# Block products of the last feed-forward ahead of every second weight tile, and fold loads one job earlier

## The chip, the cores and the metric

The kernel runs on one core of one Trainium2 chip. A core has TensorE (PE, matmuls), VectorE (DVE), ScalarE (ACT), GpSimd (POOL) and SyncE (SP); each takes its instructions in a fixed order of its own, and they wait for one another by semaphores. Sixteen DMA engines move data between HBM and the on-chip memory SBUF; matmul results lie in PSUM. Times are microseconds (us) of the device for one execution; the time of a kernel is the median of several executions.

## The reference

A two-layer encoder over 272 tokens (16 meta tokens and 256 real ones) of width 2048, in float32. Each layer has an attention branch, a Fourier branch, gates, and a convolutional feed-forward of width 5632:

```
for i in range(DEPTH):                       # DEPTH = 2
    h = _rmsnorm(h_stream, norm_mix[i])
    proj = h @ w_in[i]                       # q | k | v | f | ga | gf
    ...
    h_stream = h_stream + merged @ w_out[i]
    h2 = _rmsnorm(h_stream, norm_ffn[i])
    up = h2 @ w_up[i]                        # 2048 -> 2 * 5632
    u_gate = _dwconv3_centred(up[..., :D_FF], w_conv[i], b_conv[i])
    u_val = up[..., D_FF:]
    h_stream = h_stream + (jax.nn.silu(u_gate) * u_val) @ w_down[i]
return h_stream[:, N_META:]
```

## The kernel before

**Weight tiles.** All weights pass through the core once, in chunks of 512 KB, numbered in the order of their use. SP loads a chunk into a buffer `raw` (`load_raw`, L264; four buffers, and up to two more, `raw5`). To get float32 accuracy from PE's shorter format, `split_w` makes two parts of it: ACT casts it to `wh` (L306), and DVE makes `wl`, the chunk minus `wh` (L308). There are three buffers each of `wh` and `wl`. `next_split` brings the splits two chunks ahead of the one that PE uses. The activations are split in the same way, into a and b, and PE adds up wh·a, wh·b and wl·a. A buffer is free when PE has used it for the last time.

**Weight tiles and products.** `group` (L377 to L379) uses a chunk as a *weight tile*: 24 matmuls, 272 columns wide, or 258 in the last feed-forward (in its few `uv` groups 16, L373 and L374, half of them twice as wide). The last feed-forward (layer 1) mixes these with *block products*: the value half of `up` and the down projection are worked out by block formulas that save multiplications and use sums and differences of weights, prepared earlier and kept in HBM. `products` (L1467) uses a chunk as a product: six matmuls 512 columns wide, four with `wh`, two with `wl`. There are 252 of them. The small operands of products, `opnd`, are made from activations (`make`, `split_unit`) by a cast on ACT (L1315) and a difference on DVE (L1316), at times after sums (L1401, L1405, L1407, L1525, L1526); there are two buffers of them. Finished sums of products are handed out of PSUM by L1386, L1446 or L1448.

**The gate.** Each `ug` group has four weight tiles, and at its end stands `conv_gate`: for each of two halves `u` (DVE L1302), then the convolution (ACT L1304, DVE L1306 and L1307), then silu (ACT L1308); where the value half comes from products, four small transposes on PE (L1502, `ps_vr`) and two multiplications on DVE (L1504) follow.

**What sets the order.** The 120 chunks of the `ug`, `uv` and `t` groups of the last feed-forward are counted by t. A table of due numbers says how many products must have been begun by which t, and `mix` stands that many ahead of a tile:

```
DUE = ((0, 0), (7, 0), (43, 96), (62, 112), (64, 112), (98, 196), (100, 196), (118, 252), (120, 252))
```

Between the points of the table it goes in a straight line: two or three products ahead of every tile, fewer than one for t from 43 to 62. Side work is cut into steps: after every second group of matmuls `step` issues the next piece of the generators that stand in line (`push(generator, wait)`; the number that a generator yields is the steps until its next piece). The order in which an engine takes its instructions is then fixed by a planner that looks at the whole program, and may bring some rows of an engine forward where it reckons with a wait; what it did is seen in the rows below.

**Folds.** In the feed-forward of layer 0, `prepare` makes folded weights for layer 1: POOL loads a chunk (`wi`, L541), DVE makes eight sums and differences of its blocks into `wo` (L540), POOL stores `wo` to HBM (`fw`). A job has seven steps; the load of job n is issued two jobs ahead of its work. Loads and results take turns in seven buffers. Later jobs of the same loop (sums) have their loads four jobs ahead.

**Key statistics.** In layer 1, `kstats` runs beside the `v` group: sums of squares (PE `ps_ss`, DVE L948), a power on POOL (L518), `dk` on DVE (L994), and `ps_kb` on PE (L997).

Of the kernel before, what the change touches and what calls it, by code (L numbers as in the profile page):

```python
# [10 lines left out]
F32 = mybir.dt.float32  # L11
# [5 lines left out]
P = 128  # L17
# [15 lines left out]
CW = 4  # L33
MG = 2
# [127 lines left out]
def encoder_kernel(ctx, tc, xT, params, consts, bmat, cfold, csign, w_fl, w_f64c, w_in, w_abr, w_four, w_f64, w_out, w_up, w_down, w_vn, w_dn, w_dt, out):  # L162
# [13 lines left out]
    for l in range(DEPTH):  # L176
# [13 lines left out]
        for half in range(2):  # L190
            for kind, j in BRANCH_ORDER[half]:
                w, off, n = {"ga": (w_in, IN_GA, KT), "gf": (w_in, IN_GF, KT), "s": (w_four, 0, 8), "a": (w_abr, 0, 8)}[kind]
# [20 lines left out]
    def due(t):  # L213
        (t0, d0), (t1, d1) = next(v for v in zip(DUE, DUE[1:]) if v[0][0] <= t < v[1][0])
        return d0 + (d1 - d0) * (t - t0) // (t1 - t0)

    chunks, folded, streamed, mix, summed, stage, small_w = [], set(), set(), {}, {}, {}, {}
    t, done = 0, 0
    for key, chs in order:
        for j, ch in enumerate(chs):  # L220
            n = 0
            if key[0] == 1 and key[1] in ("t", "ug", "uv"):
                n = due(t) - done
                t += 1
            if n:
                mix[key, j] = n
                for s, p, k in PRODUCTS[done:done + n]:
                    if p in (3, 4, 5, 6):
                        summed[len(chunks)] = (min(s, len(VSETS)), (3, 0, 1, 2)[p - 3], k)
                    streamed.add(len(chunks))  # L230
                    chunks.append(pchunks[done])
                    done += 1
                first_mix = min(first_mix, len(chunks) - n) if done > n else len(chunks) - n
            if key[:2] == (0, "s"):
                folded.add(len(chunks))
            if key[:2] == (1, "t"):
                streamed.add(len(chunks))
            if key[1] in BRANCH:
                stage[len(chunks)] = key[0]
                if key[1] == "gf" and j == 0:  # L240
                    small_w[len(chunks) + KT // CW] = (key[0], key[2])
            chunks.append(ch)
# [71 lines left out]
    def push(gen, wait=0):  # L314
        shadow.append([wait, gen])
# [197 lines left out]
    def bc2(ap):  # L513
        return _rep(ap, 2)

    def pow_half(out, src):
        n = src.shape[1]
        nc.gpsimd.tensor_tensor(out, src, mhalf[:, :n], op=ALU.pow)  # L518
# [20 lines left out]
    def prepare(pool):  # L539
        tt = lambda *v, **kw: tc.keep_in_program_order(nc.vector.tensor_tensor(*v, **kw))  # L540
        dma = lambda *v: tc.keep_in_program_order(nc.gpsimd.dma_start(*v))  # L541
        tile_ = lambda n: pool.tile([P, CW, MG * P], F32, tag="ws", name=n, bufs=7)
        folds = [(w_fl[k], k) for k in range(KT)] + [(w_four[1, j, c], KT + 2 * j + c) for j in range(NG) for c in range(2)]
        sums = []
        for s_, f, wd, nq in ((0, fv[0], w_vn[0], NV), (len(VSETS), ft, w_dn, NQ)):
            for k in range(nq):
                sums += [(wd[h, nq * e + k], (s_, f, q, k)) for h, e, q in ((0, 0, 0), (1, 0, 2), (1, 1, 1), (0, 1, 3))]

        def fold(held, n, j):
            a, o = held[n], tile_(f"wo{n}")  # L550
            for q, op in ((0, ALU.add), (1, ALU.subtract)):
                for c in range(2):
                    half = (lambda t_, e: t_[:, 2 * c:2 * c + 2, e * P:(e + 1) * P]) if j < KT else (lambda t_, e: t_[:, 2 * e + c])
                    tt(half(o, q), half(a, 0), half(a, 1), op=op)
                    yield 1
            dma(fw[j], o)

        def sum_up(held, n, s_, f, q, k):
            x, y = held[n], held[n + (1, -2, 1, -1)[q]]
            for c in (0, 2):  # L560
                tt(x[:, c:c + 2], x[:, c:c + 2], y[:, c:c + 2], op=ALU.add)
                yield 1
            dma(f[q, k], x)
            ready_sums.add((s_, q, k))

        for jobs, ahead, work in ((folds, 2, lambda h, n, to: fold(h, n, to)), (sums, 4, lambda h, n, to: sum_up(h, n, *to))):
            held = {}
            for n in range(len(jobs) + ahead):
                if n < len(jobs):
                    held[n] = tile_(f"wi{n}")  # L570
                    dma(held[n], jobs[n][0])
                left = 7 - n % 4 // 3
                if n >= ahead:
                    for v in work(held, n - ahead, jobs[n - ahead][1]):
                        left -= v
                        yield v
                yield left
# [56 lines left out]
    for l in range(DEPTH):  # L634
        last = l == DEPTH - 1
# [6 lines left out]
        with tc.tile_pool(name=f"mix{l}", bufs=1) as mp:  # L642
# [23 lines left out]
            def ut(name):  # L666
                return mp.tile([P, T], F32, tag="u", name=name, bufs=2)
# [275 lines left out]
            def sums_t(dst, blocks):  # L943
                n = len(blocks)
                ss = psum.tile([P, 512], F32, tag="aux", name="ps_ss")
                for i in range(n):
                    nc.tensor.transpose(ss[:, i * P:(i + 1) * P], blocks[i], ident)
                nc.vector.tensor_reduce(dst, ss[:, 0:n * P].rearrange("p (i n) -> p i n", i=n), axis=AX.X, op=ALU.add)  # L948

            def swap(hp):  # L950
                qs = rt("qs")
                for b in range(4):
                    tc.keep_in_program_order(nc.sync.dma_start(qs[32 * b:32 * b + 32, :, :], hp[32 * (b ^ 1):32 * (b ^ 1) + 32, :, :]))
                return qs
# [6 lines left out]
            def rope(hp, qs, H, L):  # L961
                turn(hp, qs)
                nc.scalar.copy(H, hp)
                yield 1
                nc.vector.tensor_tensor(L, hp, H.bitcast(F32), op=ALU.subtract)
# [16 lines left out]
            def kstats():  # L982
                kss = small.tile([P, 2, 3], F32, tag="kss", name="kss")
                for m in range(NKV):
                    sums_t(kss[:, m, :], (kms[m], ksq[:, m, 16:144], ksq[:, m, 144:272]))
                nc.vector.tensor_tensor(kss, kss, bc2(tok2), op=ALU.mult)
                nc.vector.tensor_scalar(kss, kss, 1.0 / HD, EPS, op0=ALU.mult, op1=ALU.add)
                rk = small.tile([P, 2, 3], F32, tag="rk", name="rk")
                pow_half(rk.rearrange("p a b -> p (a b)"), kss.rearrange("p a b -> p (a b)"))
                yield 4 if last else 6  # L990
                for kv in range(NKV):
                    dk = ut("dk")
                    for i, (a, b) in enumerate(BLK):
                        nc.vector.tensor_scalar(dk[:, a:b], mask[:, a:b], rk[:, kv, i:i + 1], None, op0=ALU.mult)  # L994
                    yield 5
                    pk = psum.tile([P, 512], F32, tag="aux", name="ps_kb")
                    nc.tensor.matmul(pk[:, :T], ones, dk, start=True, stop=True)  # L997
                    nc.vector.tensor_tensor(kp[:, kv, :], kp[:, kv, :], pk[:, :T], op=ALU.mult)
                yield 3
                qs = swap(kp)  # L1000
                yield 8
                yield from rope(kp, qs, kH, kL)
                hold["keys"] = True

            push(kstats(), 6 if last else 4)
            if last:
                slots = fold_setup()
                push(fold_ahead(slots), 2)
# [186 lines left out]
            for i in range(4):  # L1195
# [3 lines left out]
                if last:  # L1199
                    if i in (0, 2):  # L1200
                        until(hold, "vt" if i == 0 else "fold")
                        for t_, n in ((qH, "q1"), (qL, "q2")):
                            o = Q_AT[l][t_ is qL][i // 2]
                            t = mp.tile([P, 4 * T + o], F32R, tag=n + "ab"[i // 2], name=n)
                            t_.append(t[:, o:o + 4 * T].rearrange("p (h t) -> p h t", t=T))
                elif i == 0:
                    until(hold, "vt")
                    until(hold, "fold")
                    for t_, n in ((qH, "q1"), (qL, "q2")):
                        o = Q_AT[l][t_ is qL][0]  # L1210
                        t = mp.tile([P, NH * T + o], F32R, tag=n, name=n)[:, o:o + NH * T].rearrange("p (h t) -> p h t", t=T)
# [74 lines left out]
        with tc.tile_pool(name=f"ffn{l}", bufs=1) as fp:  # L1286
# [3 lines left out]
            if not last:  # L1290
                slow[2] = 0
                push(prepare(fp), 8)
# [334 lines left out]
```

## Time and profile before

| | |
|---|---|
| median of 3 runs | 2507.89 us (2507.48 to 2508.49) |
| profiled execution | 2508.71 us, its span 2506.9 us |
| PE busy | 2497.2 us |
| DVE busy | 1987.6 us |
| ACT busy | 1340.5 us |
| POOL busy | 205.5 us |

The span runs from the first to the last instruction that the profile shows; 1.8 us of the profiled execution lie outside it. "Busy" counts the time in which an engine works on at least one instruction. A row of the timeline gives the start in the span, the duration, the engine, the line of the kernel, the operation with output and inputs, how many instructions stand in the row, and in brackets the idle time before it with what ended that. Durations of neighbouring rows may overlap, since an engine begins an instruction before the last one has fully ended. In the list of waits a row gives the waiting instruction, what it waited for, and the us in total, the number of times and the longest.

### The profile page before, as it was taken

Reading aid. Unit: us, or ns where it says so; the run is one execution under the profiler, and the core shown is the slowest. Engines: PE = TensorE matmul, PEld = TensorE weight load, DVE = VectorE, ACT = ScalarE, POOL = GpSimd, SP = SyncE. Lnnn points to the kernel's source line nnn. Section 1 sums busy time; section 2 is a strip of 40 time slices with the busy share of each in tenths; the row PEclk is TensorE's granted clock in tenths of the full one; section 3 lists DMA queues with packets and bytes.
Section 4 is the critical chain, followed back from the end, with each engine's and each line's share of the span. In section 5 each row is a group of like instructions: output and inputs, shape, how many; then the busy total and the mean of one; then the engine's idle time right before and its main releaser. Section 6 shows DMA issues by size and latency. Waiting matters only on the chain.

```text
span 2506.9 us, 47935 instructions
## 1 busy us (share of the span) xinstructions
PE 2497.2 (100%) x18848; PEld 2417.8 (96%) x18848; DVE 1987.6 (79%) x3155; ACT 1340.5 (53%) x1913; POOL 205.5 (8%) x394
## 2 busy tenths in 40 slices
PE   9999999999999999999999999999999999999999
PEld 9999999999999999999999999999988899999887
DVE  7687866778878667888778887666888787898898
ACT  6455444554444334444445555444676665666665
POOL 0000000012212222222200000000000000000000
PEclk9999999999999999999999999999999999999999
DMA  6544557879999999999975547888778886788887
GB/s 249 167 153 166 189 194 243 264 261 377 386 338 381 396 388 385 391 383 389 386 282 200 199 153 241 267 259 272 246 266 293 296 294 236 262 283 290 280 302 272
DMA packets 194803, 706.85 MB, mean 282 GB/s; under 512 B 22145, under 2 KB 27393, under 8 KB 194321
## 3 DMA queue, kind: packets, MB, share of 16 engines
q1 hardware_dynamic: 146768, 517.09, 58.0%
q0 software_dynamic: 46368, 184.57, 21.2%
q8 instruction: 147, 2.41, 0.4%
q10 hardware_dynamic: 1440, 2.13, 0.2%
q14 instruction: 80, 0.65, 0.1%
HBM read 623.32 MB, written 111.15 MB: 293 GB/s over the span
## 4 chain that ended last, share of the span: by engine, by line
PE 98%; DMA 1%; DVE 1%; issue 0%; ACT 0%; POOL 0%; SPq 0%; DVEq 0%
PE ps_p L1467 14%; PE ps_ug L379 7%; PE ps_ug L377 7%; PE ps_ug L378 7%; PE ps_d L379 3%; PE ps_d L377 3%; PE ps_d L378 3%; PE ps_uv L379 3%; PE ps_uv L377 3%; PE ps_uv L378 3%; PE ps_gf L377 3%; PE ps_ga L377 2%; PE ps_ga L378 2%; PE ps_o L379 2%; PE ps_o L377 2%; PE ps_ga L379 2%
## 5 line engine op out<-in xcount | busy, mean ns | idle before, releaser
L306 ACT CAST wh<-raw 128x1024 fp32r<-128x1024 f32 (+1 forms) x961 | 998.3, 1044 | 885.1 <-PE ps_ug L378 201.7
L308 DVE TENSOR_TENSOR wl<-raw,wh 128x1024 fp32r<-128x1024 f32 (+1 forms) x961 | 1159.0, 1217 | 388.6 <-ACT wh L306 378.4
L377 PE MATMUL ps_ug<-xHL,wh 128*128 128x272 f32 (+1 forms) x1408 | 400.4, 285 | 0.0
L379 PE MATMUL ps_ug<-xHL,wl 128*128 128x272 f32 (+1 forms) x1408 | 398.7, 284 | 0.0
L378 PE MATMUL ps_ug<-xHL,wh 128*128 128x272 f32 (+1 forms) x1408 | 398.5, 283 | 0.0
L377 PEld LDWEIGHTS ps_ug<-xHL,wh 128*128 128x128 f32 x1408 | 264.9, 188 | 3.2
L378 PEld LDWEIGHTS ps_ug<-xHL,wh 128*128 128x128 f32 x1408 | 264.5, 188 | 3.2
L379 PEld LDWEIGHTS ps_ug<-xHL,wl 128*128 128x128 f32 x1408 | 264.3, 188 | 1.1 <-DVE wl L308 0.4
L1467 PE MATMUL ps_p<-wh,opnd 128*128 128x512 f32 x816 | 222.1, 392 | 0.0
L379 PE MATMUL ps_uv<-xHL,wl 128*128 128x272 f32 x704 | 202.0, 287 | 0.7 <-DVE wl L308 0.7
L379 PE MATMUL ps_d<-gHL,wl 128*128 128x272 f32 x704 | 201.7, 287 | 0.0
L377 PE MATMUL ps_uv<-xHL,wh 128*128 128x272 f32 x704 | 201.3, 286 | 0.0
L377 PE MATMUL ps_d<-gHL,wh 128*128 128x272 f32 x704 | 201.1, 286 | 0.0
L378 PE MATMUL ps_uv<-xHL,wh 128*128 128x272 f32 x704 | 200.6, 285 | 0.0
L378 PE MATMUL ps_d<-gHL,wh 128*128 128x272 f32 x704 | 200.6, 285 | 0.0
L1467 PEld LDWEIGHTS ps_p<-wh,opnd 128*128 128x128 f32 x816 | 148.3, 188 | 28.7 <-ACT wh L306 0.2
L377 PE MATMUL ps_ga<-xHL,wh 128*128 128x272 f32 (+1 forms) x512 | 147.8, 289 | 0.0
L540 DVE TENSOR_TENSOR wi<-wi,wi 128x512 f32<-128x512 f32 x224 | 147.0, 685 | 0.0
L377 PE MATMUL ps_gf<-xHL,wh 128*128 128x272 f32 (+1 forms) x512 | 146.8, 287 | 0.0
L379 PE MATMUL ps_o<-mH,wl 128*128 128x272 f32 (+1 forms) x512 | 145.8, 285 | 0.0
L377 PE MATMUL ps_o<-mH,wh 128*128 128x272 f32 (+1 forms) x512 | 145.5, 284 | 0.0
L378 PE MATMUL ps_ga<-xHL,wh 128*128 128x272 f32 (+1 forms) x512 | 145.4, 284 | 0.0
(381 smaller groups left out, 5957.8 us busy)
## 6 DMA issues: line engine op xcount, KB each, us to landing
raw<-in_w_up SPq DMA_DIRECT2D x288, 512.0 KB, 6.4
raw<-in_w_in SPq DMA_DIRECT2D x191, 512.0 KB, 3.7
raw<-in_w_down SPq DMA_DIRECT2D x88, 512.0 KB, 7.1
wi<-in_w_dn POOLq DMA_DIRECT2D x80, 512.0 KB, 9.6
ft<-wi POOLq DMA_DIRECT2D x80, 512.0 KB, 7.8
raw<-ft SPq DMA_DIRECT2D x80, 512.0 KB, 4.5
raw<-in_w_out SPq DMA_DIRECT2D x64, 512.0 KB, 4.2
raw<-fv SPq DMA_DIRECT2D x64, 512.0 KB, 4.6
```

The costliest lines, as they stand in the source:

```text
L306: nc.scalar.copy(h[:, a:b], r[:, a:b])
L308: nc.vector.tensor_tensor(lo[:, a:b], r[:, a:b], h[:, a:b].bitcast(F32), op=ALU.subtract)
L377: nc.tensor.matmul(o, h[:, c, sl], a, start=kt == 0, stop=False)
L378: nc.tensor.matmul(o, h[:, c, sl], b, start=False, stop=False)
L379: nc.tensor.matmul(o, lo[:, c, sl], a, start=False, stop=kt == nk - 1)
L540: tt = lambda *v, **kw: tc.keep_in_program_order(nc.vector.tensor_tensor(*v, **kw))
L1467: nc.tensor.matmul(ps[h], x, w[:, 512 * h:512 * h + 512], start=fresh and (s_, q) in BEGIN and first, stop=(s_, q) in END and end, skip_gr ...
```

## The change

In the last feed-forward, the number of products ahead of a tile is now taken for two tiles at once: ahead of an even t stand those due at t + 1, ahead of an odd t none. Where the table rises fastest this makes five to seven ahead of every even tile in place of two or three ahead of each. The total stays 252.

Loads of folds are issued three jobs ahead of their work in place of two; since the work keeps its distance to the load by this count, the work of a fold and its store come one job later. The buffers for it are nine in place of seven. In the key statistics of layer 1, the first piece comes after 5 steps in place of 6, and the wait behind it is 5 in place of 4, so the later pieces keep their place.

```
@@ the order of chunks
             n = 0
             if key[0] == 1 and key[1] in ("t", "ug", "uv"):
-                n = due(t) - done
+                n = due(t + 1 - t % 2) - done
                 t += 1
@@ prepare
-        tile_ = lambda n: pool.tile([P, CW, MG * P], F32, tag="ws", name=n, bufs=7)
+        tile_ = lambda n: pool.tile([P, CW, MG * P], F32, tag="ws", name=n, bufs=9)
...
-        for jobs, ahead, work in ((folds, 2, lambda h, n, to: fold(h, n, to)), (sums, 4, lambda h, n, to: sum_up(h, n, *to))):
+        for jobs, ahead, work in ((folds, 3, lambda h, n, to: fold(h, n, to)), (sums, 4, lambda h, n, to: sum_up(h, n, *to))):
@@ kstats
-                yield 4 if last else 6
+                yield 5 if last else 6
...
-            push(kstats(), 6 if last else 4)
+            push(kstats(), 5 if last else 4)
```

Below, tiles go by their number in the order of use (`wh806` and `wl806` are the two parts of chunk 806); the number behind the underscore is only the planner's.

DVE in the last feed-forward, at the end of `ug` group 16. Before, 803 and 807 are weight tiles, 804 to 806 and 808 are products:

```order
L308 TENSOR_TENSOR wl804_26863<-raw804_26717,wh804_26862 128x1024
L1504 TENSOR_TENSOR act_22652<-cv_26825,ps_vr_26830 128x256
L308 TENSOR_TENSOR wl805_26877<-raw805_26747,wh805_26876 128x1024
L1525 TENSOR_TENSOR XT_70<-act_22652 128x256
L1526 TENSOR_TENSOR act_22652<-act_22652 128x2x128
L308 TENSOR_TENSOR wl806_26905<-raw806_26759,wh806_26904 128x1024
L1316 TENSOR_TENSOR opnd_26910<-XT_70,opnd_26910 128x256
L308 TENSOR_TENSOR wl807_26920<-raw807_26774,wh807_26919 128x4x256
L308 TENSOR_TENSOR wl808_26932<-raw808_26786,wh808_26931 128x1024
```

Now 801 to 805 are products, 806 and 807 weight tiles, and the next products begin with 808:

```order
L308 TENSOR_TENSOR wl804_26863<-raw804_26717,wh804_26862 128x1024
L1504 TENSOR_TENSOR act_22652<-cv_26825,ps_vr_26830 128x256
L308 TENSOR_TENSOR wl805_26875<-raw805_26729,wh805_26874 128x1024
L1525 TENSOR_TENSOR XT_70<-act_22652 128x256
L1316 TENSOR_TENSOR opnd_26880<-XT_70,opnd_26880 128x256
L1526 TENSOR_TENSOR act_22652<-act_22652 128x2x128
L308 TENSOR_TENSOR wl806_26890<-raw806_26744,wh806_26889 128x4x256
L308 TENSOR_TENSOR wl807_26902<-raw807_26756,wh807_26901 128x4x256
```

The splits of 804 and 805 keep their place; the operand of the products from 808 on (`opnd_26910`, now `opnd_26880`), made from what L1525 writes, now comes ahead of the split of 806.

ACT at the same place, before:

```order
L306 CAST wh804_26862<-raw804_26717 128x1024
L1315 CAST opnd_26853<-act_22652 128x256
L306 CAST wh805_26876<-raw805_26747 128x1024
L1308 ACTIVATE cv_26825<-cv_26825 128x256
L306 CAST wh806_26904<-raw806_26759 128x1024
L306 CAST wh807_26919<-raw807_26774 128x4x256
L1315 CAST opnd_26910<-XT_70 128x256
L306 CAST wh808_26931<-raw808_26786 128x1024
```

and now:

```order
L306 CAST wh804_26862<-raw804_26717 128x1024
L306 CAST wh805_26874<-raw805_26729 128x1024
L1308 ACTIVATE cv_26825<-cv_26825 128x256
L1315 CAST opnd_26880<-XT_70 128x256
L306 CAST wh806_26889<-raw806_26744 128x4x256
L306 CAST wh807_26901<-raw807_26756 128x4x256
L306 CAST wh808_26921<-raw808_26786 128x1024
```

The cast of the operand moved from behind the casts of 806 and 807 to ahead of both.

PE at the end of group 17. Before, 832 to 834 are products, 835 a weight tile:

```order
L1467 MATMUL ps_p10_22999<-wh834_27469,opnd_27333 128x512
L1467 MATMUL ps_p11_23000<-wh834_27469,opnd_27333 128x512
L1467 MATMUL ps_p10_22999<-wh834_27469,opnd_27333 128x512
L1467 MATMUL ps_p11_23000<-wh834_27469,opnd_27333 128x512
L1467 MATMUL ps_p10_22999<-wl834_27470,opnd_27333 128x512
L1467 MATMUL ps_p11_23000<-wl834_27470,opnd_27333 128x512
L377 MATMUL ps_1_ug_14_0_27402<-xHL_71,wh835_27481 128x258
L378 MATMUL ps_1_ug_14_0_27402<-xHL_71,wh835_27481 128x258
L377 MATMUL ps_1_ug_14_1_27403<-xHL_71,wh835_27481 128x258
L378 MATMUL ps_1_ug_14_1_27403<-xHL_71,wh835_27481 128x258
L379 MATMUL ps_1_ug_14_0_27402<-xHL_71,wl835_27482 128x258
```

Now 829 to 833 are products, 834 and 835 weight tiles, and the next products begin with 836:

```order
L377 MATMUL ps_1_ug_14_0_27402<-xHL_71,wh834_27451 128x258
L378 MATMUL ps_1_ug_14_0_27402<-xHL_71,wh834_27451 128x258
L377 MATMUL ps_1_ug_14_1_27403<-xHL_71,wh834_27451 128x258
L378 MATMUL ps_1_ug_14_1_27403<-xHL_71,wh834_27451 128x258
L1502 MATMUL ps_vr_27658<-cst_73,vR_22653 128x128
L1502 MATMUL ps_vr_27658<-cst_73,vR_22655 128x128
L1502 MATMUL ps_vr_27658<-cst_73,vR_22653 128x128
L1502 MATMUL ps_vr_27658<-cst_73,vR_22655 128x128
L1467 MATMUL ps_p10_22999<-wl833_27440,opnd_27303 128x512
L1467 MATMUL ps_p11_23000<-wl833_27440,opnd_27303 128x512
L1467 MATMUL ps_p10_22999<-wh836_27481,opnd_27429 128x512
L1467 MATMUL ps_p11_23000<-wh836_27481,opnd_27429 128x512
```

The four `wh` matmuls of the weight tile, the transposes and two matmuls of the next product now stand ahead of its first `wl` matmul, which follows. At group 16 it goes in the same way: two matmuls of weight tile 806 stand ahead of the `wl` part of 805, two behind it, then three transposes and the four `wh` matmuls of 808.

POOL at the beginning of the folds, before:

```order
L541 DMA wi2_6943<-in_w_fl 128x1024
L541 DMA fw_66<-wo0_6945 128x1024
L541 DMA wi3_7005<-in_w_fl 128x1024
L541 DMA fw_66<-wo1_7007 128x1024
L541 DMA wi4_7063<-in_w_fl 128x1024
L541 DMA fw_66<-wo2_7065 128x1024
L541 DMA wi5_7125<-in_w_fl 128x1024
```

and now:

```order
L541 DMA wi2_6943<-in_w_fl 128x1024
L541 DMA wi3_6999<-in_w_fl 128x1024
L541 DMA fw_66<-wo0_7001 128x1024
L541 DMA wi4_7057<-in_w_fl 128x1024
L541 DMA fw_66<-wo1_7059 128x1024
L541 DMA wi5_7119<-in_w_fl 128x1024
```

Each load now stands ahead of one store more.

## The prediction

> **What bounds the kernel now.** I read the head of the page first, then the chain of waits, then the list of what TensorE (PE) waited for, and last the windows by stage.
>
> ```profile
> span 2506.9 us, 47935 instructions
> PE 2497.2 (100%) x18848; PEld 2417.8 (96%) x18848; DVE 1987.6 (79%) x3155; ACT 1340.5 (53%) x1913; POOL 205.5 (8%) x394
> PEclk9999999999999999999999999999999999999999
> PE 98%; DMA 1%; DVE 1%; issue 0%; ACT 0%; POOL 0%; SPq 0%; DVEq 0%
> ```
> ```profile
> PE ps_f L444 <- ACT wh L306: 4.5, 1, 4.5
> PE ps_uv L379 <- DVE wl L308: 0.7, 1, 0.7
> PE ps_kb L997 <- DVE dk L994: 0.5, 1, 0.5
> PE ps_uv L374 <- DVE wl L308: 0.3, 1, 0.3
> ```
> ```profile
> 1826.00:2042.00 216.00, 215.68 (x1226) 188.48 (x1225) 180.83 (x218) 149.44 (x185) 0.00 (x0) 1.00 0.85 291
> 2090.00:2330.00 240.00, 240.00 (x1573) 219.63 (x1572) 206.11 (x273) 155.76 (x197) 0.00 (x0) 1.00 0.79 270
> ```
>
> PE is the whole span: 2497.2 of 2506.9 us, 98% of the chain, always at full clock. In the list of waits only the last row lies in the last feed-forward. In the windows (columns: length, busy PE, weight loads, VectorE (DVE), ScalarE (ACT), GpSimd (POOL), clock, DMA share, GB/s) PE has no gap in 240 us, but DVE stands at 206 of 240 (86%). So no reordering can win more than these few tenths there; it can only lose, where DVE or ACT, whose orders are fixed, deliver a tile late. The change spreads DVE's work less evenly against PE's needs, so I looked at the place where DVE has most to do: the end of a `ug` group, here group 16. First PE, then DVE, then two ACT rows.
>
> ```profile
> 2194.78 0.29 PE L379 MATMUL ps_ug<-xHL,wl 128*128 128x258 f32 x1
> 2194.91 0.60 PE L1502 MATMUL ps_vr<-cst,vR 128*128 128x128 f32 x4
> 2195.26 1.18 PE L1467 MATMUL ps_p<-wh,opnd 128*128 128x512 f32 x4
> ...
> 2196.74 1.09 PE L1467 MATMUL ps_p<-wh,opnd 128*128 128x512 f32 x4
> 2197.67 0.62 PE L1467 MATMUL ps_p<-wl,opnd 128*128 128x512 f32 x2
> 2198.12 0.28 PE L377 MATMUL ps_ug<-xHL,wh 128*128 128x258 f32 x1
> 2198.24 0.28 PE L378 MATMUL ps_ug<-xHL,wh 128*128 128x258 f32 x1
> ```
> ```profile
> 2195.11 0.43 DVE L1302 TENSOR_TENSOR u<-ps_ug,rstdB 128x258 f32<-128x258 f32 x1
> 2195.45 0.48 DVE L1306 SCALAR_TENSOR_TENSOR cv<-u,prm,cv 128x256 f32<-128x256 f32 x1
> 2195.97 0.48 DVE L1307 SCALAR_TENSOR_TENSOR cv<-u,prm,cv 128x255 f32<-128x255 f32 x1
> 2196.37 1.22 DVE L308 TENSOR_TENSOR wl<-raw,wh 128x1024 fp32r<-128x1024 f32 x1
> 2197.50 0.48 DVE L1306 SCALAR_TENSOR_TENSOR cv<-u,prm,cv 128x256 f32<-128x256 f32 x1
> 2197.90 0.42 DVE L1504 TENSOR_TENSOR act<-cv,ps_vr 128x256 f32<-128x256 f32 x1
> 2198.23 0.48 DVE L1307 SCALAR_TENSOR_TENSOR cv<-u,prm,cv 128x255 f32<-128x255 f32 x1
> 2198.62 0.43 DVE L1316 TENSOR_TENSOR opnd<-act,opnd 128x256 fp32r<-128x256 f32 x1
> 2198.96 1.23 DVE L308 TENSOR_TENSOR wl<-raw,wh 128x1024 fp32r<-128x1024 f32 x1
> 2200.09 0.42 DVE L1504 TENSOR_TENSOR act<-cv,ps_vr 128x256 f32<-128x256 f32 x1
> 2200.42 1.23 DVE L308 TENSOR_TENSOR wl<-raw,wh 128x1024 fp32r<-128x1024 f32 x1
> ```
> ```profile
> 2201.08 2.09 ACT L306 CAST wh<-raw 128x1024 fp32r<-128x1024 f32 x2 [1.66 <-issue]
> 2203.08 0.40 ACT L1315 CAST opnd<-XT 128x256 fp32r<-128x256 f32 x1
> ```
>
> PE gives the steps: a product takes 2198.12 - 2196.74 = 1.38 us and wants its `wl` 0.93 after its start; a matmul of a weight tile takes 0.12, so a tile of 24 takes 2.88 and wants `wl` 0.24 after its start. Crossing from product to weight tile costs nothing (2197.67 to 2198.12 is two products' matmuls). DVE gives its own: a row costs 0.08 less than its duration, since the next begins early (split 1.14, convolution row 0.40, 256-wide row 0.34).
>
> **The change part by part.** Its largest edit puts five or six products ahead of every even tile. Arithmetic, splits and loads are the same in number; only their order moves. Between groups a burst is harmless: DVE splits at 1.14 against 1.38. At a group's end DVE also has the convolution's rows, some 3 us, before the weight tile behind the burst. Time zero is the burst's start, which now directly follows the group's last matmul (2194.91 in the rows above, the transposes having moved behind).
>
> Group 16 (burst 801 to 805). DVE's rows stay in the same order up to the split of 805, so by the rows above: `u` 0.20, third split 1.46, fourth 4.05, fifth 5.51 to 6.74. PE ends the four `wh` matmuls of 805 at 4 x 1.38 + 0.93 = 6.45 and now wants `wh806`. On ACT, `opnd_26880` stands ahead of that cast, and its source is what L1525 writes, which DVE reaches behind the fifth split: 5.51 + 1.14 = 6.65, done 7.07. Then ACT needs 0.42 for the operand and 1.05 for `wh806` (half of 2.09): 8.55, so PE waits 2.1 us. PE goes on with 2 matmuls of 806, 2 of 805, 2 of 806 and 3 transposes (0.24 + 0.46 + 0.24 + 0.27), to 9.76, and wants `wh808`, whose cast is two more behind: 10.65, a wait of 0.9. Together 3.0; I take **2.9**. Before, `opnd_26910` stood behind the casts of 806 and 807, and held nobody.
>
> An ordinary end, group 17 (burst 829 to 833), in whose DVE rows there is also this:
>
> ```profile
> L1316 DVE TENSOR_TENSOR opnd<-XT,opnd 128x384 fp32r<-128x384 f32 x16 | 8.8, 552 | 0.0
> L1525 DVE TENSOR_TENSOR XT<-act 128x256 f32<-128x256 f32 x7 | 3.0, 423 | 0.1
> L1386 DVE SCALAR_TENSOR_TENSOR res<-ps_p,sgn,res 128x512 f32<-128x512 f32 x28 | 20.6, 746 | 0.8 <-PE ps_p L1467 0.8
> 2204.81 1.05 ACT L306 CAST wh<-raw 128x1024 fp32r<-128x1024 f32 x1 [0.27 <-PE ps_p L1467]
> ```
>
> Fourth split 3.71, L1504 4.85, L1316 5.18, L1525 5.65, fifth split 5.99 to 7.22, L1526 7.13, split of weight tile 834 from 7.47 to 8.70. PE: 6.45, four `wh` matmuls of 834 0.48, four transposes 0.35, two `wl` of 833 0.46, two of 836 0.46: it wants `wl834` at 8.20, and waits **0.45**. The two of 836 have a bound of their own: a third buffer comes free at 6.45, and with about 0.2 to start (an estimate from the gaps of casts that PE releases, as in the last row) and 1.05 the cast is there at 7.8.
>
> The same addition for the other ends gives, by first tile of the burst: 622 0.4, 710 0.3, 725 0.15, 787 0.2, 815 0.35, 842 0.05, 856 0.05, 870 0.15, 884 0.8, 896 0.2, 909 0.1, 925 0.6, 942 0.25, 958 0.3: 3.9. All waits: 2.9 + 0.45 + 3.9 = **+7.25**. Each term is good to some 0.3 either way, and below nothing there is no room. Of the 0.3 that PE waited at L374 I strike all: **-0.3**.
>
> Weight loads. Five products ask for 512 KB per 1.38 us, 380 GB/s, against the 270 to 291 of the windows. What ACT's casts waited for in the last feed-forward, the largest group first, and what a load takes to land (the last number):
>
> ```profile
> ACT wh L306 <- PE ps_ug L378: 99.2, 54, 2.4
> ```
> ```profile
> raw<-in_w_up SPq DMA_DIRECT2D x102, 512.0 KB, 4.9
> ```
>
> They wait for PE to free buffers; no group of that list names a load, so loads have slack. A burst of five draws about half a tile more ahead of the mean than one of three (0.9 us at the mean rate). I take 0; if the cover is gone, at most 0.9 at each of 16 ends, none of which is in the sum.
>
> Longer fold lead. The one PE wait behind it is the 0.7 above, when DVE stood for a fold's load and the split behind it came late:
>
> ```profile
> 644.89 0.39 PE L379 MATMUL ps_uv<-xHL,wl 128*128 128x272 f32 x1 [0.67 <-DVE wl L308]
> ```
> ```profile
> 638.08 0.43 DVE L540 TENSOR_TENSOR wo<-wi 128x256 f32<-128x256 f32 x1 [3.74 <-DMA wi<-in_w_four]
> ```
>
> With a load one job (seven steps) earlier DVE doesn't wait there: **-0.8**: the 0.67, and a matmul that took 0.1 more than its neighbours' 0.28 to 0.29; between 0 and -0.9. POOL now issues one more load ahead of the first store; a store comes a job later, and its readers lie far behind. The Trainium skill (DMA: Bandwidth & Descriptors, Issuing engines are not separate DMA queues) says that all issuers' transfers interleave on the same 16 engines; by it the earlier load is paid for by another transfer, and the term would be 0. No run here separates it.
>
> Key statistics of layer 1. PE's small matmuls come one step earlier, but
>
> ```profile
> 1338.43 1.15 DVE L994 TENSOR_SCALAR dk<-cst,rk 128x16 f32<-128x16 f32 x6 [1.22 <-POOL rk L518]
> ```
>
> `dk` waits for POOL's power, whose input DVE makes in unchanged order: **0**, at best the 0.5 of `ps_kb`.
>
> Sum: 7.25 - 0.3 - 0.8 = +6.1. The profiled execution took 2508.71, 0.82 above the median; it would become 2514.8, the median 2507.9 + 6.1 = **2514.0**.
>
> **The rivals.** Below 0.2% (5 us) a measurement of this kernel hardly tells a change.
>
> *Not slower: DVE keeps up.* Only the queue at group 16 costs, the fifteen other ends nothing: +2.9 - 1.1 = +1.8, 2509.7. For it speaks that PE's order brings matmuls forward exactly there, and that my lateness is mostly under 0.5. It decides if an end costs under (5.0 + 1.1 - 2.9) / 15 = 0.21 us rather than the 0.29 reckoned. Without that queue too (the operand not needing L1525's columns) 2506.8 remains.
>
> *Slower by more: the lateness runs through.* If DVE's rows in the burst take their durations, not 0.08 less, twelve of them make each end 0.96 later; less 0.3 of slack where there was some, 14 x 0.65 = 9 more, 2523. Against it: the quoted rows overlap throughout.
>
> *Faster.* Longer runs of one kind would have to spare 5 us at some 60 joints, 80 ns each. The joints cost nothing and the granted clock is 1.00. The Trainium skill (Perfetto Trace Analysis, Matmul Optimizations) says that matmuls should run back to back in batches because power scales with use; PE already does, in both orders, as the full window shows.
>
> **How the numbers follow.** Forecast (2511 to 2517) 0.44; only group 16 costs 0.25; nothing waits 0.12; lateness runs through 0.15; faster 0.04. Slower by over 0.2% (above 2512.9) is the run-through and 0.38 of the forecast's 0.44: 0.53. Within 0.2%: 0.25 + 0.12 + 0.06 = 0.43. The range leaves out half of "nothing waits" and over half of the run-through: 2506.5 to 2521.
>
> **What would show it.** In the list of PE's waits, `wh` from L306 twice after group 16 (2 and 0.9 us); `wl` from L308 at the ends of groups 12 to 18, none over 1 us; no 3.7 us wait of L540 for `in_w_four` near 638. I am wrong if PE waits inside bursts away from group ends, for loads, or not at all.

## The result, and the profile after

| | before | after |
|---|---|---|
| median (6 runs each) | 2507.58 us (2507.16 to 2508.49) | 2517.44 us (2516.45 to 2519.14) |
| profiled execution | 2508.71 us | 2517.44 us |
| its span | 2506.9 us | 2515.7 us |

The changed kernel takes 1.0038 times as long (95% interval 1.0028 to 1.0049): 9.9 us slower, where 6.1 were forecast. The time lies just above the 2511 to 2517 that the prediction gave to its own mechanism. The page's head and the chain of the changed kernel:

```profile
span 2515.7 us, 47941 instructions
PE 2502.8 (99%) x18848; PEld 2414.9 (96%) x18848; DVE 1987.3 (79%) x3155; ACT 1335.5 (53%) x1913; POOL 204.2 (8%) x394
PEclk9999999999999999999999999999999999999999
PE 96%; DVE 2%; ACT 1%; issue 0%; DMA 0%; POOL 0%; ACTq 0%; DVEq 0%; POOLq 0%
```

The same matmuls at the same clock; the chain now has 2% of DVE and 1% of ACT. Where the time came in can be read by setting the start of the same matmul in both traces side by side (changed kernel less the one before, in the two profiled executions):

| stretch | later by |
|---|---|
| first 57 us (the first loads) | +1.2 |
| folds, 602 to 652 | -0.9 |
| key statistics of layer 1, 1297 to 1348 | -0.7 |
| last feed-forward | +9.1 |
| end | +8.7 |

So the whole loss lies in the last feed-forward. The list of PE's waits there hardly shows it, though. This is that list for the changed kernel, from 1830 us on, and under it the same list for the weight loads (PEld), which PE runs ahead of its matmuls:

```profile
PE ps_p L1467 <- ACT wh L306: 1.7, 5, 0.5
PE ps_p L1467 <- DVE wl L308: 0.5, 2, 0.3
PE ps_uv L374 <- DVE wl L308: 0.3, 2, 0.2
```
```profile
PEld ps_p L1467 <- ACT wh L306: 5.8, 13, 0.9
PEld ps_p L1467 <- DVE wl L308: 5.4, 17, 0.7
PEld ps_uv L374 <- DVE wl L308: 2.1, 4, 0.6
PEld ps_p L1467 <- DVE opnd L1316: 0.4, 1, 0.4
PEld ps_ug L377 <- ACT wh L306: 0.4, 1, 0.4
PEld ps_ug L379 <- DVE wl L308: 0.2, 1, 0.2
```

and the weight loads before:

```profile
PEld ps_uv L374 <- DVE wl L308: 0.7, 1, 0.7
PEld ps_ug L379 <- DVE wl L308: 0.4, 2, 0.2
PEld ps_t L1548 <- DVE wl L308: 0.2, 1, 0.2
PEld ps_p L1467 <- ACT wh L306: 0.2, 1, 0.2
```

PE's list has 2.5 us, that of the weight loads 14.3 after against 1.5 before. A third measure is the distance from each matmul's start to the next one's, its *pitch*. A place where it is over 0.12 us longer than the median for its width I call a *stop*. Before, the last feed-forward has one; now it has 22. Together they are 6.7 us longer than the median, and the matmul behind each is 0.11 slow once more (below, the slow restart), 2.4: 9.1 us. The one stop before came to 0.6, so the stops make 8.5 of the 9.1 us lost; the rest lies in pitches that are longer by less than 0.12. Only 3.2 us of this is idle time by PE's rows. The rest, 5.9 us, is 0.27 a stop, and the smallest stops show it: 0.14 and 0.11 with an idle time of 0.00.

How a stop comes about is seen at the prediction's example, the end of `ug` group 17. PE, DVE and ACT of the changed kernel; the burst 829 to 833 begins at 2249.54:

```profile
2255.17 1.08 PE L1467 MATMUL ps_p<-wh,opnd 128*128 128x512 f32 x4
...
2256.92 0.71 PE L1467 MATMUL ps_p<-wl,opnd 128*128 128x512 f32 x2
2258.11 0.73 PE L1467 MATMUL ps_p<-wh,opnd 128*128 128x512 f32 x2 [0.48 <-ACT wh L306]
2258.68 0.41 PE L379 MATMUL ps_ug<-xHL,wl 128*128 128x258 f32 x2
```
```profile
2253.32 1.22 DVE L308 TENSOR_TENSOR wl<-raw,wh 128x1024 fp32r<-128x1024 f32 x1
2254.49 0.42 DVE L1504 TENSOR_TENSOR act<-cv,ps_vr 128x256 f32<-128x256 f32 x1
2254.82 0.55 DVE L1316 TENSOR_TENSOR opnd<-XT,opnd 128x384 fp32r<-128x384 f32 x1
2255.29 0.42 DVE L1525 TENSOR_TENSOR XT<-act 128x256 f32<-128x256 f32 x1
2255.63 1.22 DVE L308 TENSOR_TENSOR wl<-raw,wh 128x1024 fp32r<-128x1024 f32 x1
```
```profile
2254.36 1.98 ACT L306 CAST wh<-raw 128x1024 fp32r<-128x1024 f32 x2
2257.01 1.05 ACT L306 CAST wh<-raw 128x1024 fp32r<-128x1024 f32 x1 [0.67 <-DVE wl L308]
2257.96 0.51 ACT L1315 CAST opnd<-XT 128x384 fp32r<-128x384 f32 x1
```

PE had used `wh833` four times by 2256.09. But the cast of `wh836` into that buffer begins at 2257.01, since DVE reads `wh833` too: it forms `wl833` from it, from 2255.63 to 2256.85, behind the gate's rows. So the late split holds the buffer, the buffer holds the cast, and the cast holds PE: the first matmul of 836 could have begun at 2257.38 (2256.92 plus two pitches of 0.23), and begins at 2258.11. The chain of the changed kernel goes the same way, from DVE's split over ACT's cast to PE:

```profile
2255.71 1.15 DVE wl L308
...
2257.01 1.05 ACT wh L306
2258.07 0.04 issue
2258.11 0.73 PE ps_p L1467 x2
```

### The profile page after: what moved, and what is told of

The parts are those of the page before. It is cut to its first block, busy times and chain, and to the rows that moved or that the text cites. A ratio compares the mean times of both kernels' runs of the same rounds, so it can differ in the third digit from the quotient of the medians.

```text
span 2515.7 us, 47941 instructions
## 1 busy us (share of the span) xinstructions
PE 2502.8 (99%) x18848; PEld 2414.9 (96%) x18848; DVE 1987.3 (79%) x3155; ACT 1335.5 (53%) x1913; POOL 204.2 (8%) x394
## 4 chain that ended last, share of the span: by engine, by line
PE 96%; DVE 2%; ACT 1%; issue 0%; DMA 0%; POOL 0%; ACTq 0%; DVEq 0%; POOLq 0%
PE ps_p L1467 12%; PE ps_ug L379 7%; PE ps_ug L377 7%; PE ps_ug L378 7%; PE ps_d L379 3%; PE ps_uv L379 3%; PE ps_uv L377 3%; PE ps_d L377 3%; PE ps_uv L378 3%; PE ps_d L378 3%; PE ps_gf L377 2%; PE ps_ga L377 2%; PE ps_ga L378 2%; PE ps_o L379 2%; PE ps_o L377 2%; PE ps_ga L379 2%
```

## The experiments

**Products alone, and the side edits (folds and key statistics) alone.** The first kernel has only the new place of the products:

```
-                n = due(t) - done
+                n = due(t + 1 - t % 2) - done
```

> Only the products move; folds and key statistics as before. In the trace of the changed kernel, the last feed-forward alone is 9.4 us longer (sum of matmul pitches over their medians, 14.1 against 4.75), the fold stretch 0.94 shorter and the key statistics 0.68 shorter. Theory (stops of PE at the group ends): 2507.6 + 9.4 = 2517.0, a little slower than or equal to the whole change within the noise of the start. Rival (the two side edits cost something in the last feed-forward): under 2513.

Measured 2516.76 us (before, on the same chip: 2507.68, over 27 runs), ratio 1.0035 (1.0021 to 1.0049): 9.1 us slower, with the same 22 stops. The second has the rest of the change only:

```
-        tile_ = lambda n: pool.tile([P, CW, MG * P], F32, tag="ws", name=n, bufs=7)
+        tile_ = lambda n: pool.tile([P, CW, MG * P], F32, tag="ws", name=n, bufs=9)
...
-        for jobs, ahead, work in ((folds, 2, lambda h, n, to: fold(h, n, to)), (sums, 4, lambda h, n, to: sum_up(h, n, *to))):
+        for jobs, ahead, work in ((folds, 3, lambda h, n, to: fold(h, n, to)), (sums, 4, lambda h, n, to: sum_up(h, n, *to))):
...
-                yield 4 if last else 6
+                yield 5 if last else 6
...
-            push(kstats(), 6 if last else 4)
+            push(kstats(), 5 if last else 4)
```

> Fold lead and key statistics alone, products as before. Theory: the two gains stand by themselves, 0.94 + 0.68 = 1.6 us: 2506.0 (2505.3 to 2507.0), and the last feed-forward's excess stays at 4.7 us. Rival: the longer fold lead only moves the wait, 2507.6.

Measured 2507.71 against 2507.68, ratio 0.9999 (0.999 to 1.0008): no gain is seen. The interval, from 2.5 us faster to 2.0 slower, would still hide 1.6 us, but the whole change, which has these edits, wasn't faster than products alone either (2517.44 and 2516.76). The products-alone kernel says where the 1.6 us of the two traces can have come from. Its folds are those of before, and its trace too was 0.9 and 0.7 us ahead of that of before in the two stretches. DVE's waits for fold loads from 500 to 1250 us, in the execution before and in the products-alone kernel, which have the same order there:

```profile
DVE wo L540 <- DMA wi<-in_w_four: 11.3, 7, 3.7
DVE wo L540 <- DMA wi<-in_w_fl: 2.2, 3, 1.1
```
```profile
DVE wo L540 <- DMA wi<-in_w_four: 7.8, 6, 2.2
DVE wo L540 <- DMA wi<-in_w_fl: 0.9, 2, 0.7
```

The longest wait is 2.2 in place of 3.7, and PE has no wait behind it, nor at `ps_kb`. So of two executions with the same order there, one has PE's 0.7 and 0.5 and the other doesn't: they are no fixed cost of the kernel. With the longer lead DVE's waits for `in_w_four` and `in_w_fl` are gone from the list altogether, and no gain shows in the time.

**Same bursts, other place.** The products due for two tiles ahead of the odd tile:

```
-                n = due(t + 1 - t % 2) - done
+                n = due(min(t + t % 2, 119)) - done
```

Bursts of five to seven stand ahead of the second and fourth tile of a group, so that one weight tile stands between the gate and the next burst.

> The whole change, but the products due for two tiles stand ahead of the odd tile (the second and fourth of a group) in place of the even one: bursts of the same five to seven, the same loads, but a weight tile stands between a group's end and the next burst. Theory (DVE and ACT are late because the gate's work at the group's end meets a burst): the stops go, the last feed-forward loses under 3 us against before, 2506 to 2509. Rival (a burst of five or more is too fast for loads, casts or splits wherever it stands): 2515 to 2518 again.

Measured 2509.15, ratio 1.0005 (0.9996 to 1.0014), with 6 stops. The weight loads' waits for `wh` and `wl`:

```profile
PEld ps_p L1467 <- ACT wh L306: 1.8, 4, 1.1
PEld ps_uv L374 <- DVE wl L308: 0.4, 2, 0.2
PEld ps_t L1548 <- DVE wl L308: 0.4, 1, 0.4
PEld ps_p L1467 <- DVE wl L308: 0.3, 1, 0.3
```

Bursts of this length, with their loads of 512 KB per 1.38 us, cost little in themselves: the 6 stops take 2.4 us with their slow restarts, where 22 took 9.1. What costs most is that a burst follows a group's end at once. Nor do longer runs of one kind win anything that can be seen.

**A fourth buffer for `wh`, or for `wl`.** In the last feed-forward every fourth chunk takes its `wh` from a buffer of its own:

```
+            more = st["stage"] == DEPTH and i >= first_mix and (i - first_mix) % 4 == 3
-            splits[i] = tuple(weight_rows(wp.tile([P, CW * CS], F32R, tag=t, name=f"{t}{i}"), i in streamed) for t in ("wh", "wl"))
+            splits[i] = tuple(weight_rows(st["pool"].tile([P, CW * CS], F32R, tag=t + "5", name=f"{t}{i}", bufs=1) if more and t in ('wh',)
+                                          else wp.tile([P, CW * CS], F32R, tag=t, name=f"{t}{i}"), i in streamed) for t in ("wh", "wl"))
```

> The whole change, with a fourth buffer for wh in the last feed-forward (every fourth chunk there has a buffer of its own). In the changed kernel 11 of 22 stops stand ahead of a product's first wh matmul, 3.9 us and 1.2 us of slow restarts. Theory (the cast is late because its buffer came free late): these go, 2517.4 - 5 = 2512.5 (2511 to 2514). Rival (the cast is late for its raw load or for ACT's order): 2516 to 2518.

Measured 2508.17, ratio 1.0003 (0.9994 to 1.0012), with 2 stops: far more than expected, since the stops ahead of `wl` went as well. PE's order is the planner's and changed with it: at the end of group 17 the `wl` matmuls of 833 again follow directly on its `wh` matmuls, and three matmuls of 836, in place of two, stand ahead of the first `wl` matmul of 834. The fourth buffer is at work there: 836 now takes the buffer of 832, and its cast, the second of these two, runs while DVE still reads `wh833`:

```profile
2249.77 2.15 ACT L308 CAST wh<-raw 128x1024 fp32r<-128x1024 f32 x2
```
```profile
2250.71 1.22 DVE L310 TENSOR_TENSOR wl<-raw,wh 128x1024 fp32r<-128x1024 f32 x1
```

But the order helps as well. The four transposes now stand ahead of the burst, and DVE's split of 833 begins 5.24 us after the burst's start, where it was 6.09. How much of what was won is the buffer's, and how much the new order's, wasn't separated. All weight loads' waits that are left (lines are two higher here):

```profile
PEld ps_ug L381 <- DVE wl L310: 0.9, 3, 0.5
PEld ps_p L1469 <- DVE wl L310: 0.7, 3, 0.3
PEld ps_p L1469 <- ACT wh L308: 0.4, 1, 0.4
PEld ps_uv L376 <- DVE wl L310: 0.2, 1, 0.2
```

The same with `'wl'` in place of `'wh'`:

> The whole change, with a fourth buffer for wl in the last feed-forward, wh with three. A fourth wh buffer brought 2508.2. Theory (it is wh's buffer that comes free late, and splits on DVE are late through it): most of the 22 stops stay, 2515 to 2518. Rival (any one buffer more lets the splits run further ahead): 2508 to 2511.

Measured 2517.35, ratio 1.0039 (1.0024 to 1.0054), again 22 stops, at the same places. So it isn't buffers in general. (Before, on the chip of this run and the next two: 2507.65, over 21 runs.)

```profile
PEld ps_p L1469 <- ACT wh L308: 5.6, 12, 0.9
PEld ps_p L1469 <- DVE wl L310: 5.2, 17, 0.7
```

**Less work for DVE at the gate.**

```
-                    nc.vector.scalar_tensor_tensor(cv[:, a:T], u[:, a - 1:T - 1], wc(0), cv[:, a:T], op0=ALU.mult, op1=ALU.add)
-                    nc.vector.scalar_tensor_tensor(cv[:, lo2:T - 1], u[:, lo2 + 1:T], wc(2), cv[:, lo2:T - 1], op0=ALU.mult, op1=ALU.add)
+                    if not last:
+                        nc.vector.scalar_tensor_tensor(cv[:, a:T], u[:, a - 1:T - 1], wc(0), cv[:, a:T], op0=ALU.mult, op1=ALU.add)
+                        nc.vector.scalar_tensor_tensor(cv[:, lo2:T - 1], u[:, lo2 + 1:T], wc(2), cv[:, lo2:T - 1], op0=ALU.mult, op1=ALU.add)
```

> The whole change without the convolution's two outer taps in the last feed-forward (L1306 and L1307 are left out there, so the gate sees only the middle tap): 1.6 us of DVE less at each group's end, buffers as they are. Prediction's step (DVE is late at the ends): the stops ahead of wl matmuls go with their price, 10 of 22, some 4 us, and those ahead of wh stay: about 2513.5. Rival 1 (DVE sets all stops): 2508 to 2509.5. Rival 2 (wh's buffer sets all): 2516 to 2518.

Measured 2512.54, ratio 1.0019 (1.001 to 1.0028), with 11 stops: about half the loss. The time is near the expected 2513.5, but for another reason. The eight stops between 2000 and 2340 us (at the ends of groups 4, 5, 12 to 14, 17 and 18) all went, those ahead of `wh` too, which were to stay, and ACT no longer waits for DVE's split in the list of its waits, where the changed kernel has

```profile
ACT wh L306 <- DVE wl L308: 4.3, 6, 2.1
```

Five of the six stops ahead of 2000 us stayed, beside the early `uv` groups, and six of eight behind 2340 us.

So between 2000 and 2340 us either cure is nearly enough: without DVE's rows the split comes in time and frees `wh`'s buffer; with a fourth buffer the cast needn't wait for it (one stop, ahead of a `wl`, is left there). By these rows the stops there come from both together; PE's order differs a little in both kernels, so neither cure was tried quite by itself. What else the 11 others need wasn't tried singly; with the fourth `wh` buffer one stop is left in their stretches.

**The same buffer without the bursts.** Products as before, the side edits, a fourth `wh` buffer.

> Products as before, fold lead and key statistics as changed, a fourth wh buffer in the last feed-forward. Theory (before, PE is stopped once there, and little else is left): the excess falls from 3.8 us to about 3, the time from 2507.7 to 2507.0, not to be told from before. Rival (slack in wh also opens something before): under 2505.

Measured 2509.39, ratio 1.0006 (0.9998 to 1.0015): no stop is left at all, and no wait of the weight loads, yet nothing is won. In its trace the mean pitch of the 128x512 matmuls, without the few that are far above the median, is 230.2 ns, against 229.5 in the side-edits kernel, and that of the 128x258 ones 119.24 against 119.06: with some 1500 and 5200 of them about 2 us, which eats the 0.6 of the one stop. Why the pitch is longer stays open: the two kernels differ in the buffers' place in memory and in PE's order at some hundred matmuls, and they ran on different chips, and none of this was tried by itself. No version beat the kernel before.

## Why the prediction was right or wrong

**Direction and place: right.** PE had no gaps to win from, and a burst behind a group's end is too much for the splits; the run with the bursts at odd tiles shows that it is mainly the place, and not their length. Loads at 0 was right as well: ACT waited for a load twice, 1.4 us in all, and PE has no stop within 10 us behind either.

**Group 16, 2.9 us: wrong.** The failing step is "its source is what L1525 writes". ACT and DVE of the changed kernel there:

```profile
2201.76 0.39 ACT L1315 CAST opnd<-XT 128x256 fp32r<-128x256 f32 x1
2202.05 3.19 ACT L306 CAST wh<-raw 128x1024 fp32r<-128x1024 f32 x3
```
```profile
2203.77 0.42 DVE L1525 TENSOR_TENSOR XT<-act 128x256 f32<-128x256 f32 x1
```

The cast of the operand ran two us before L1525: both touch the tile XT, in different columns. Up to the next burst PE lost 0.4 us, by pitches against their medians. The name of a tile in a row isn't a dependence.

**An ordinary end, 0.45 us at group 17: mechanism half right, size too small.** DVE's own times came as worked out: the fifth split was to begin 5.99 and end 7.22 after the burst's start, and ran from 6.09 to 7.31. What failed is "a third buffer comes free at 6.45": that is PE's last use, but DVE's split reads the same buffer and ends at 7.31. ("A buffer is free when PE has used it for the last time", in the part on the kernel, is too short in the same way.) So PE stopped ahead of 836, where I had nothing, and the wait for `wl834` behind it vanished in that; 8.70 less 8.20 would have been 0.50 for it, not 0.45. Up to the next burst PE lost 0.8.

**All ends, 4.35 us without group 16: a term was missing.** Measured 9.1 us in 22 stops. In idle time, in which the terms were worked out, the ends came to less than forecast: 2.8 us, and 0.4 more beside the early `uv` groups. Two things were missing. Each stop costs 0.27 beyond its idle time, so that one of "0.05" costs 0.3; that is 5.9 us in all. And four bursts beside the early `uv` groups (637, 652, 659, 681), which I had at nothing, have five stops of 0.25 to 0.5 us with the slow restart, 1.7 of the 9.1. That the forecast of 7.25 for all waits came near the measured 9.1 was luck: too much idle time, the 2.9 of group 16 above all, stood in for the price of a stop. The 0.3 struck at L374 did go from its place, but the new stops put 0.3 on the same line of PE's list again.

**Folds, -0.8 us: not borne out; key statistics, 0: as forecast.** No gain was seen, though the interval would hide this much. The failing step is that a wait seen in one profiled execution belongs to the kernel. That execution lay 0.82 above the median, and its two odd waits, 0.7 and 0.5 us, are more than that. The Trainium skill (DMA: Bandwidth & Descriptors, Issuing engines are not separate DMA queues) gave 0 for this term, and no gain was seen; but whether that rule decided it isn't shown. DVE's waits for fold loads, 13.5 us, are gone with the longer lead, and ACT's waits for weight chunks from 500 to 1250 us came to 18.0 in place of 18.9, so no transfer is seen to pay for them; and PE had only the one wait behind them in any case.

**Rivals.** "DVE keeps up" needed under 0.21 us per end and was out: the stops away from group 16 cost more than twice that. "The lateness runs through" (2523) was out, since DVE's rows overlapped as in the rows before. "Faster" by longer runs of one kind was out: with hardly a stop in them, the odd-tile bursts took 2509.15, not less than before.

## What to carry to other kernels

A buffer is free when its last reader is done, and where one engine's result is read both by PE and by the engine that makes the second half, the slower of the two frees it: work out both. Count the stops of a PE that never idles, not only their length, and look for them in the waits of the weight loads. A wait of less than a us that stands once in one profiled execution need not be a gain to be had, least of all where that execution lies above the median.

## What the runs showed that was not expected

A stop of PE has a price of its own, about 0.27 us: 0.16 in the distance to the next matmul, with idle time added one to one (idle 0.05 gave 0.21, 0.14 gave 0.31, 0.22 gave 0.38, 0.31 gave 0.48, 0.48 gave 0.65), and 0.11 on the matmul behind it. The weight load that normally runs beside the matmul ahead of it can't begin before its tile is there; at group 17 it begins with the late matmul itself:

```profile
2258.11 0.30 PEld L1467 LDWEIGHTS ps_p<-wh,opnd 128*128 128x128 f32 x2 [0.91 <-ACT wh L306]
```

Its wait, 0.91, is longer than PE's 0.48. That the exposed load is the 0.16 and 0.11 was only argued from such rows, not tried by itself.
